# Other buffers, another order of loads and an earlier start for the gate sums of a hybrid decoder layer

## The chip, the cores and the metric

The kernel runs on one core of a Trainium2 chip. The core has a matrix engine (TensorE, "PE" in the profile, with its weight loads as "PEld"), three engines for elementwise work (VectorE "DVE", ScalarE "ACT", GpSimd "POOL") and SyncE ("SP"), which here issues nearly all transfers between the device memory (HBM) and the on-chip memory (SBUF). Each engine works through its own instructions in order; semaphores order them between engines. The metric is the device time of one execution in microseconds (us): lower is better. Times given as "median" are over several executions; the profile shows one execution.

## The reference, cut to what matters

One layer over 512 tokens of width 2048, with a conditioning vector `c`:

```
mod = silu(c) @ w_ada + b_ada              # (1, 3*2048)
shift, scale, gate = split(mod, 3)
h = rms_norm(x, norm_g) * (1 + scale) + shift
u_a, v_a, g_a, q_b, k_b, v_b, g_b, f_b = split(h @ w_in)
y_a = chunked_spatial_gating(gelu(u_a), gelu(v_a), ln_v, w_s, b_s) * silu(g_a)    # branch A
y_b = forgetting_attention(q_b, k_b, v_b, f_b, b_f) * silu(g_b)                    # branch B
y = concat(y_a, y_b) @ w_out
x = x + gate * y
return rms_norm(x, final_g)
```

The change concerns the vector `gate`: 2048 sums over 2048 products of `silu(c)` with the last third of `w_ada` (16 MB of weights). It is not needed before the output projection, near the end.

## The kernel before

**Matrix products.** Everything is float32. A product is made of three passes: each factor is split into a high part (ScalarE rounds, line 131) and a low part (VectorE, or GpSimd in the first stage, subtracts, line 132), and TensorE adds hi x hi, lo x hi and hi x lo. `w_tile` (line 119) makes one weight tile: a buffer of tag `raw` (four buffers of 128 partitions x 4 KB), its load on SP's queue, and the two halves in tags `whi` and `wlo` (two buffers each). `newest_w[0]` (lines 101, 125) always holds the newest such load.

**Stages, in order of time.** (1) shift and scale, `h`, and the first projections beside them, up to about 188 us. (2) `va_products` (line 740): the values of branch A, 16 weight tiles, to about 283 us. (3) the group "ga" (four tiles) and `v_group(0)` (eight half-size tiles), with the spatial mixing of branch A between them. (4) groups of q, k, gate and values of branch B, four tiles each, with the attention of four heads at a time laid between them. (5) the output projection `unit(0)`, `unit(1)`: seven products of half matrices each, in place of eight, which needs sums and differences of quarters of `w_out`. These are made beforehand on GpSimd from loads and written to a scratch tensor `tsum` in HBM: `sum_step(0, k)` for unit 0 (buffers `vs`, `pth`, `ptl`) and `sum_part(1, k, p)` for unit 1 (buffers `wsp`).

**What is laid between.** After each weight tile of stages 2 to 5 the loop calls `tick()` (line 135), which takes one entry of `slots` (attention and mixing steps) and one entry of `fillers`. A tick is thus the time of one weight tile on TensorE and of what is laid in it. Fillers are `spatial_weights`, then eight `sum_step(0, k)` with an empty entry behind each (17 entries: 16 ticks of stage 2 and the first of "ga"). In stage 4 come the gate sums: 32 calls of `gate_step(g, i)` (line 596; `g` one of four column blocks, `i` one of eight pairs of row blocks), with `gate_sum(g)` (line 660) some steps after the last of its block; then the 16 `sum_part` calls.

**The gate steps.** `gate_step` takes a buffer of tag `raw`, loads 512 KB of `w_ada` on SP, and on GpSimd does for each of two row blocks a product with `silu(c)` (line 605, or 603 for the first) and an addition to `gate` (line 606). `gate_sum` adds the 128 partitions with a matrix of ones on TensorE and adds the bias, from a tile `bg` of tag `raw`.

**Order.** The Tile framework orders the instructions of each engine when the program is built: by priority (the order of the program, which `high_priority` shifts ahead; `w_tile` does), by the readiness that a model of time gives, and by free buffers. A tile of a tag waits for one of the tag's buffers to come free. `tc.issue_after(ins)` puts what is traced in it behind `ins` in the queue of that engine. Nothing in the queue of SP overtakes anything: a transfer that waits for a buffer holds up all behind it.

**The buffers `wsp`.** Two of 4 KB per partition. First they hold the split spatial weights (`wsp[0]` for the mixing of heads 0 to 3, `wsp[1]` for 4 to 7, line 777), later the tiles of `sum_part`, and in `unit(1)` two result tiles.

Of the kernel before, what the change touches and what calls it, by code (L numbers as in the profile page):

```python
# [8 lines left out]
F32 = mybir.dt.float32  # L9
# [6 lines left out]
P = 128  # L16
# [11 lines left out]
def trunk_kernel(  # L28
# [17 lines left out]
    nc = tc.nc  # L46

    ada_r = w_ada[0].rearrange("(kb p) (s n) -> p kb s n", p=P, s=3)
# [5 lines left out]
    wp = ctx.enter_context(tc.tile_pool(name="wp", bufs=2))  # L54
# [4 lines left out]
    def bank(tag, name):  # L59
        if tag == "x":  # L60
            tag = "bbbc"[turn[0] % 4]
            turn[0] += 1
        return ps.tile([P, 512], F32, tag=tag, name=name, bufs={"mm": 4, "b": 3, "c": 1}[tag])
# [37 lines left out]
    newest_w = [None]  # L101
# [12 lines left out]
    fillers = []  # L114
# [102 lines left out]
    gate = gp_.tile([P, 4, 512], F32, name="gate")  # L217
# [141 lines left out]
    for q, (k0, nk) in enumerate(CH):  # L359
# [10 lines left out]
        for si, sid in enumerate(order):  # L370
# [9 lines left out]
            for kk in range(k0, k0 + nk, st_k):  # L380
                for gi, (segs, bl) in enumerate(grp):
                    hi, lo = w_tile(
                        segs, kk, st_k, name=f"st{q}_{sid}_{gi}_{kk}", pri=0,
# [29 lines left out]
    pb = ctx.enter_context(tc.tile_pool(name="pb", bufs=1))  # L413
# [15 lines left out]
    wsp = [pb.tile([P, 4, 2, P], F32R, name=f"wsp{i}", tag="wsp", bufs=2) for i in range(2)]  # L429
# [163 lines left out]
        split(fsplit[:, 0, :], fsplit[:, 1, :], f3)  # L593


    def gate_step(g, i):
        ga = wp.tile([P, 2, 512], F32, tag="raw", name=f"gate{g}_{i}", bufs=4)
        nc.sync.dma_start(ga, ada_r[:, 2 * i : 2 * i + 2, 2, g * 512 : (g + 1) * 512])
        for j in range(2):
            kk = 2 * i + j  # L600
            a = gate[:, g, :]
            if kk == 0:
                nc.gpsimd.tensor_scalar(a, ga[:, j], sc[:, 0:1], None, ALU.mult)
            else:
                nc.gpsimd.tensor_scalar(ga[:, j], ga[:, j], sc[:, kk : kk + 1], None, ALU.mult)  # L605
                nc.gpsimd.tensor_tensor(a, a, ga[:, j], ALU.add)  # L606
# [8 lines left out]
    def sum_step(u, k):  # L615

        js = slice((k % 2) * 512, (k % 2) * 512 + 512)
        w = wout_r[:, :, u * 1024 : (u + 1) * 1024].rearrange("p k (s n) -> p k s n", s=2)
        if k % 2:
            a = [pb.tile([P, 2, 512], F32, tag=t, name=f"ts{t}{u}_{k}") for t in ("pth", "ptl")]  # L620
        else:
            o = pb.tile([P, 4, 512], F32, tag="vs", name=f"ts{u}_{k}")
            a = [o[:, 0:2, :], o[:, 2:4, :]]
        nc.sync.dma_start(a[0], w[:, 8 + k])
        nc.sync.dma_start(a[1], w[:, k])
        b11, b12, b21, b22 = (a[z // 2][:, z % 2, :] for z in range(4))
        for z, (dst, l, r) in enumerate((
            (b11, b12, b11), (b12, b12, b22), (b22, b22, b11), (b21, b21, b22),
        )):
            nc.gpsimd.tensor_tensor(dst, l, r, ALU.subtract)  # L630
        if k % 2:
            nc.sync.dma_start(tsum[u][k // 2][:, 0:2, js], a[0])
            nc.sync.dma_start(tsum[u][k // 2][:, 2:4, js], a[1])
        else:
            nc.sync.dma_start(tsum[u][k // 2][:, :, js], o)
# [24 lines left out]
    def gate_sum(g):  # L660
        gsl = slice(2 * D + g * 512, 2 * D + (g + 1) * 512)
        bg = wp.tile([P, 512], F32, name=f"bg{g}", tag="raw", bufs=4)
        nc.sync.dma_start(bg, b_ada[:, gsl].broadcast_to([P, 512]))
        gp = bank("x", f"gp{g}")
        nc.tensor.matmul(gp, ones, gate[:, g, :], start=True, stop=True)
        nc.vector.tensor_tensor(gate[:, g, :], gp, bg, ALU.add)
# [73 lines left out]
    def va_products():  # L740
        va.extend([[pb.tile([P, 512], F32, tag="qstk", bufs=8, name=f"va{t}_{g}") for g in range(2)] for t in range(NT)])
        vst = [pb.tile([P, 2, 6], F32, name=f"vst{t}") for t in range(NT)]
        for g in range(2):
            banks = [bank("x" if g else "mm", f"va{g}_{t}") for t in range(NT)]
            for k in range(0, KB, 2):
                hi, lo = w_tile([(V0 + g * 512, 512)], k, 2, name=f"va{g}_{k}")
                mm_toks(banks, 512, hi, lo, hh, hl, [k, k + 1], 0, KB - 1)
                tick()
            for t in range(NT):
                nc.scalar.activation(va[t][g], banks[t], AF.Gelu)  # L750
                nc.vector.bn_stats(vst[t][:, g, :], va[t][g])
        for t in range(NT):
            mv = pb.tile([P, 2], F32, name=f"mv{t}")
            nc.vector.bn_aggr(mv, vst[t].rearrange("p a b -> p (a b)"))
            rs_ = pb.tile([P, 1], F32, name=f"rsv{t}")
            rsqrt_of(rs_, mv[:, 1:2], 1.0)
            mvs.append(mv)
            rvs.append(rs_)
# [37 lines left out]

    fillers.append(spatial_weights)
    for k in range(8):
        fillers.extend([lambda k=k: sum_step(0, k), lambda: None])
    va_products()  # L800
    slots.extend([
        [c_(norm_half, 0)],
# [9 lines left out]
    gates = []  # L812
    for g in range(4):
        for i in range(8):
            gates.append(lambda g=g, i=i: gate_step(g, i))
            if g and i == 2:
                gates.append(lambda g=g: gate_sum(g - 1))
    gates.extend([lambda: None] * 2 + [lambda: gate_sum(3)])
    parts = [lambda k=k, p=p: sum_part(1, k, p) for k in range(8) for p in range(2)]
    n = 0  # L820
# [330 lines left out]
```

## Time and profile before

| | |
|---|---|
| time, median of 3 executions | 909.44 us (907.97 to 909.47) |
| the profiled execution: time | 907.83 us |
| the profiled execution: span, first to last instruction | 906.1 us |
| granted TensorE clock, mean | 0.986 of full speed |
| matmul instructions | 4408 |
| HBM read and written | 166.90 MB and 20.97 MB |

The profile page gives each engine's busy time, the span in 40 slices with the busy tenths of each, and groups of instructions by line. Beside the page, views of the trace answer narrower questions: stretches (busy time of every engine from A to B us), waits (which engine stood still, at which line, and what released it), the timeline (instructions one by one, with idle time before them and its releaser in brackets), and groups by line in a stretch. In "x<-y" x is written and y read. A matmul is drawn with a modelled end, longer than the distance to the next start, so starts tell more than ends do. The mean over the span hides the stages: each has its own bound.

The DMA slices and what the sums move:

```profile
DMA  9999997338996164544554546676676236577575
gate<-in_w_ada_dram SPq DMA_DIRECT2D x32, 512.0 KB
```

A slice is 22.65 us: the DMA engines are full in the first six, to about 136 us, dense again from the tenth to the thirteenth (stage 2 and what follows, 204 to 294 us), and at four to six tenths in most of stage 4.

### The profile page before, as it was taken

Reading aid. Unit: us, or ns where it says so; the run is one execution under the profiler, and the core shown is the slowest. Engines: PE = TensorE matmul, PEld = TensorE weight load, DVE = VectorE, ACT = ScalarE, POOL = GpSimd, SP = SyncE. Lnnn points to the kernel's source line nnn. Section 1 sums busy time; section 2 is a strip of 40 time slices with the busy share of each in tenths; the row PEclk is TensorE's granted clock in tenths of the full one; section 3 lists DMA queues with packets and bytes.
Section 4 is the critical chain, followed back from the end, with each engine's and each line's share of the span. In section 5 each row is a group of like instructions: output and inputs, shape, how many; then the busy total and the mean of one; then the engine's idle time right before and its main releaser. Section 6 shows DMA issues by size and latency. Waiting matters only on the chain.

```text
span 906.1 us, 12687 instructions
## 1 busy us (share of the span) xinstructions
PE 880.7 (97%) x4408; PEld 745.3 (82%) x4408; DVE 593.8 (66%) x982; ACT 445.5 (49%) x775; POOL 436.9 (48%) x338
## 2 busy tenths in 40 slices
PE   6999999999999999999999999999999999999995
PEld 4888888887888997778789888998897888888884
DVE  4758888473436866454686563447764679996687
ACT  5554332452213324455666554557465657655454
POOL 2365655425576359889998879444651000000001
PEclk7899999999999999999999999999999999999998
DMA  9999997338996164544554546676676236577575
GB/s 340 323 340 357 354 328 222 110 113 292 311 323 201 38 182 125 163 153 136 167 160 141 177 129 186 198 232 191 203 240 203 74 113 213 185 252 245 178 235 205
DMA packets 139712, 188.91 MB, mean 208 GB/s; under 512 B 9968, under 2 KB 103360, under 8 KB 139136
## 3 DMA queue, kind: packets, MB, share of 16 engines
q1 hardware_dynamic: 139216, 187.53, 65.0%
q8 instruction: 35, 0.57, 0.3%
q10 hardware_dynamic: 432, 0.57, 0.2%
q14 instruction: 29, 0.24, 0.1%
HBM read 166.90 MB, written 20.97 MB: 207 GB/s over the span
## 4 chain that ended last, share of the span: by engine, by line
PE 85%; DMA 5%; DVE 4%; issue 2%; ACT 2%; POOL 1%; SPq 0%; POOLq 0%; ACTq 0%; DVEq 0%
PE s L147 6%; PE s L149 6%; PE s L148 6%; PE vb L156 3%; PE vb L157 3%; PE vb L158 3%; PE va L158 3%; PE va L157 3%; PE va L156 3%; PE gb L149 3%; PE gb L148 3%; PE gb L147 3%; PE q L149 3%; PE q L148 3%; PE k L149 3%; PE q L147 3%
## 5 line engine op out<-in xcount | busy, mean ns | idle before, releaser
L605 POOL TENSOR_SCALAR gate<-gate,sc 128x512 f32<-128x512 f32 x60 | 106.4, 1784 | 23.9 <-DMA gate<-in_w_ada_dram 14.9
L132 POOL TENSOR_TENSOR wlo_st<-raw_st,whi_st 128x1024 fp32r<-128x1024 f32 (+3 forms) x36 | 68.4, 1904 | 54.2 <-ACT whi_st L131 48.0
L606 POOL TENSOR_TENSOR gate<-gate,gate 128x512 f32<-128x512 f32 x60 | 92.9, 1550 | 1.8
L147 PE MATMUL s<-hh,whi_st 128*128 128x512 f32 x224 | 88.0, 396 | 1.4 <-ACT hh L269 1.4
L148 PE MATMUL s<-hl,whi_st 128*128 128x512 f32 x224 | 87.8, 392 | 0.0
L651 POOL TENSOR_TENSOR ts<-ts 128x256 f32<-128x256 f32 x64 | 55.1, 866 | 60.4 <-DMA ts<-in_w_out_dram 57.6
L66 ACT ACTIVATE whi_p<-p 128x1024 fp32r<-128x1024 f32 x52 | 55.1, 1060 | 54.8 <-PE woZ L935 20.1
L246 DVE SCALAR_TENSOR_TENSOR acc<-ada,sc,acc 128x512 f32<-128x512 f32 x98 | 73.9, 754 | 4.9 <-DMA ada<-in_w_ada_dram 2.1
L67 DVE TENSOR_TENSOR wlo_p<-p,whi_p 128x1024 fp32r<-128x1024 f32 x52 | 63.4, 1220 | 20.2 <-ACT whi_p L66 20.1
L149 PE MATMUL s<-hh,wlo_st 128*128 128x512 f32 x224 | 76.0, 393 | 0.0
L157 PE MATMUL vb<-whi_vb,hl 128*128 128x256 f32 (+1 forms) x256 | 72.2, 285 | 0.0
L156 PE MATMUL vb<-whi_vb,hh 128*128 128x256 f32 (+1 forms) x256 | 72.0, 285 | 0.0
L158 PE MATMUL vb<-wlo_vb,hh 128*128 128x256 f32 (+1 forms) x256 | 71.3, 288 | 0.0
L978 POOL TENSOR_TENSOR sfin<-sfin,nhalf 128x1 f32<-128x1 f32 x2 | 1.5, 751 | 137.5 <-DVE sfin L1070 137.5
L131 ACT ACTIVATE whi_st<-raw_st 128x1024 fp32r<-128x1024 f32 (+3 forms) x36 | 31.2, 870 | 65.2 <-PE s L148 39.7
L147 PE MATMUL q<-hh,whi_q 128*128 128x512 f32 x128 | 50.6, 395 | 1.2 <-ACT whi_q L131 1.2
L147 PEld LDWEIGHTS s<-hh,whi_st 128*128 128x128 f32 x224 | 42.6, 191 | 10.1 <-ACT hh L269 1.5
L147 PE MATMUL k<-hh,whi_k 128*128 128x512 f32 x128 | 50.2, 392 | 0.7 <-ACT whi_k L131 0.7
L147 PE MATMUL gb<-hh,whi_gb 128*128 128x512 f32 x128 | 50.3, 393 | 0.5 <-ACT whi_gb L131 0.5
L156 PE MATMUL va<-whi_va,hh 128*128 128x512 f32 x128 | 50.3, 393 | 0.0
L148 PE MATMUL gb<-hl,whi_gb 128*128 128x512 f32 x128 | 50.2, 392 | 0.0
L148 PE MATMUL q<-hl,whi_q 128*128 128x512 f32 x128 | 50.2, 392 | 0.0
(308 smaller groups left out, 2523.4 us busy)
## 6 DMA issues: line engine op xcount, KB each, us to landing
ada<-in_w_ada_dram SPq DMA_DIRECT2D x128, 256.0 KB
gate<-in_w_ada_dram SPq DMA_DIRECT2D x32, 512.0 KB
p<-ts SPq DMA_DIRECT2D x32, 512.0 KB
p<-in_w_out_dram SPq DMA_DIRECT2D x24, 512.0 KB
raw_va<-in_w_in_dram SPq DMA_DIRECT2D x16, 512.0 KB
raw_q<-in_w_in_dram SPq DMA_DIRECT2D x16, 512.0 KB
raw_k<-in_w_in_dram SPq DMA_DIRECT2D x16, 512.0 KB
raw_gb<-in_w_in_dram SPq DMA_DIRECT2D x16, 512.0 KB
```

The source lines that it names most:

```text
L66: a = nc.scalar.activation(hi, src, AF.Copy)
L67: return a, (eng or nc.vector).tensor_tensor(lo, src, hi.bitcast(F32), ALU.subtract)
L132: (loeng or nc.vector).tensor_tensor(lo, raw, hi.bitcast(F32), ALU.subtract)
L147: nc.tensor.matmul(pt, hi[:, j, cs], hh[k], start=(k == first), stop=False)
L148: nc.tensor.matmul(pt, hi[:, j, cs], hl[k], start=False, stop=False)
L149: nc.tensor.matmul(pt, lo[:, j, cs], hh[k], start=False, stop=(k == last))
L156: nc.tensor.matmul(o, ah[k][:, tsl], hi[:, j, :], start=(k == first), stop=False)
L157: nc.tensor.matmul(o, al[k][:, tsl], hi[:, j, :], start=False, stop=False)
L158: nc.tensor.matmul(o, ah[k][:, tsl], lo[:, j, :], start=False, stop=(k == last))
L246: nc.vector.scalar_tensor_tensor(sb if kk == KB - 1 else a, ga[:, j], col, a, ALU.mult, ALU.add)
L605: nc.gpsimd.tensor_scalar(ga[:, j], ga[:, j], sc[:, kk : kk + 1], None, ALU.mult)
L606: nc.gpsimd.tensor_tensor(a, a, ga[:, j], ALU.add)
```

## The change

`gate_step` takes its tile from the two `wsp` buffers in place of the four `raw` ones, unless it is called as early; and its load, early or not, is put behind the newest weight load of that moment in SP's queue. The first four steps (`g` 0, `i` 0 to 3) are called early: they take the empty entries behind every second `sum_step(0, k)`, in the values of branch A, and stay in `raw`. The list of gate work in stage 4 then has 28 steps; every fourth entry is a `gate_sum` or empty. It has 40 entries, two more than before, so the `sum_part` calls come two ticks later.

```diff
--- before.py
+++ after.py
@@ -593,9 +593,13 @@
         split(fsplit[:, 0, :], fsplit[:, 1, :], f3)
 
 
-    def gate_step(g, i):
-        ga = wp.tile([P, 2, 512], F32, tag="raw", name=f"gate{g}_{i}", bufs=4)
-        nc.sync.dma_start(ga, ada_r[:, 2 * i : 2 * i + 2, 2, g * 512 : (g + 1) * 512])
+    def gate_step(g, i, early=False):
+        if early:
+            ga = wp.tile([P, 2, 512], F32, tag="raw", name=f"gate{g}_{i}", bufs=4)
+        else:
+            ga = pb.tile([P, 2, 512], F32, tag="wsp", name=f"gate{g}_{i}", bufs=2)
+        with tc.issue_after(newest_w[0].ins):
+            nc.sync.dma_start(ga, ada_r[:, 2 * i : 2 * i + 2, 2, g * 512 : (g + 1) * 512])
         for j in range(2):
             kk = 2 * i + j
             a = gate[:, g, :]
@@ -796,7 +800,8 @@
 
     fillers.append(spatial_weights)
     for k in range(8):
-        fillers.extend([lambda k=k: sum_step(0, k), lambda: None])
+        fillers.append(lambda k=k: sum_step(0, k))
+        fillers.append((lambda k=k: gate_step(0, k // 2, True)) if k % 2 else (lambda: None))
     va_products()
     slots.extend([
         [c_(norm_half, 0)],
@@ -812,9 +817,10 @@
     gates = []
     for g in range(4):
         for i in range(8):
-            gates.append(lambda g=g, i=i: gate_step(g, i))
-            if g and i == 2:
-                gates.append(lambda g=g: gate_sum(g - 1))
+            if g or i > 3:
+                gates.append(lambda g=g, i=i: gate_step(g, i))
+                if len(gates) % 4 == 3:
+                    gates.append((lambda g=g: gate_sum(g - 1)) if g and i in (2, 3, 4) else (lambda: None))
     gates.extend([lambda: None] * 2 + [lambda: gate_sum(3)])
     parts = [lambda k=k, p=p: sum_part(1, k, p) for k in range(8) for p in range(2)]
     n = 0
```

## The prediction

> **What bounds the kernel now.** First the page's busy row and its slices.
>
> ```profile
> span 906.1 us, 12687 instructions
> PE 880.7 (97%) x4408; PEld 745.3 (82%) x4408; DVE 593.8 (66%) x982; ACT 445.5 (49%) x775; POOL 436.9 (48%) x338
> PE   6999999999999999999999999999999999999995
> POOL 2365655425576359889998879444651000000001
> ```
>
> TensorE (PE) is the bound: 906.1 - 880.7 = 25.4 us are not drawn busy, most of them at both ends, where this change does nothing. POOL, idle half the time on average, stands at 8 and 9 tenths in one stretch only, from about 340 to 560 us, where the gate sums run. So next the view of stretches: the branch A values with the weight differences (205 to 285), the mixing (284 to 326), and the gate sums in two halves. Columns: length; PE, PEld, DVE, ACT and POOL busy with counts; clock; DMA share and GB/s.
>
> ```profile
> 205.00:285.00 80.00, 80.00 (x353) 65.53 (x352) 31.13 (x39) 21.49 (x25) 49.45 (x34) 1.00 0.89 304
> 284.00:326.00 42.00, 42.00 (x264) 38.17 (x263) 35.92 (x67) 12.78 (x20) 16.06 (x22) 1.00 0.30 76
> 340.00:460.00 120.00, 115.85 (x522) 93.02 (x521) 71.15 (x106) 61.16 (x114) 109.37 (x69) 1.00 0.49 153
> 460.00:580.00 120.00, 120.00 (x663) 104.70 (x662) 68.97 (x125) 66.95 (x134) 96.98 (x67) 1.00 0.52 157
> ```
>
> PE loses 120 - 115.85 = 4.15 us between 340 and 460 and nothing visible in the other stretches; POOL is 91% busy there, and DMA only half. The view of waits, for PE from 320 to 600 and for SP's queue from 320 to 580, names the late ones (total, times, longest):
>
> ```profile
> PE o L541 <- DVE ptl L67: 1.2, 2, 0.9
> PE q L147 <- ACT whi_q L131: 1.2, 1, 1.2
> PE k L147 <- ACT whi_k L131: 0.7, 1, 0.7
> PE gb L147 <- ACT whi_gb L131: 0.5, 1, 0.5
> PE k L149 <- DVE wlo_k L132: 0.3, 1, 0.3
> PE s L486 <- ACT s L492: 0.2, 1, 0.2
> ...
> SPq L125 <- POOL gate L606: 51.3, 18, 8.0
> SPq L598 <- POOL gate L606: 23.4, 7, 8.1
> ```
>
> PE waits for the halves of the weights (L131, L132), and SP waits 51.3 us, in 18 weight loads, for a gate sum on POOL to give back a `raw` buffer. One case on the timelines of SP and of ACT:
>
> ```profile
> 397.45 0.37 SPq L598 DMA_DIRECT2D gate<-in_w_ada_dram  x1
> 397.91 0.42 SPq L125 DMA_DIRECT2D raw_gb<-in_w_in_dram  x1
> ...
> 403.00 1.06 ACT L131 ACTIVATE whi_gb<-raw_gb 128x1024 fp32r<-128x1024 f32 x1 [3.64 <-DMA raw_gb<-in_w_in_dram]
> ```
>
> The last `raw_gb` goes out at 397.91, behind a gate load, and lands for ACT at 403.00, after PE wanted it. Two of four `raw` buffers hold gate tiles, so weights are loaded about one tile ahead, not three.
>
> What a wait costs is more than its drawn gap:
>
> ```profile
> 364.91 0.39 PE L149 MATMUL k<-hh,wlo_k 128*128 128x512 f32 x1
> 366.04 0.50 PE L147 MATMUL k<-hh,whi_k 128*128 128x512 f32 x1 [0.74 <-ACT whi_k L131]
> 366.38 0.40 PE L148 MATMUL k<-hl,whi_k 128*128 128x512 f32 x1
> 366.61 0.39 PE L147 MATMUL k<-hh,whi_k 128*128 128x512 f32 x1
> ```
>
> Undisturbed, the next matmul starts 0.23 us later (366.38 to 366.61). Here it starts 1.13 later, then 0.34 later: 0.90 + 0.11 = 1.01 us lost against 0.74 drawn, 0.27 more. The PE rows above are seven waits with 4.1 us together; with 7 x 0.27 = 1.9 that makes **6.0 us** that late weights, and the DVE and ACT work held up behind them, cost. The bounds of what can be regained are 0 and 6.0, plus about 1.5 for waits too short to be drawn as gaps.
>
> **The change part by part.**
>
> *Gate tiles leave the four `raw` buffers (28 of 32 steps).* No instruction is removed or added. The 28 loads go to `wsp`. Its two buffers hold the spatial weights until the mixing is done, which POOL's wait shows to be at 324.5, and the first gate load of before stands behind that:
>
> ```profile
> 324.50 1.92 POOL L424 MEMSET k<- 128x512 f32 x4 [14.42 <-PE mix L784]
> 325.84 0.37 SPq L598 DMA_DIRECT2D gate<-in_w_ada_dram  x1
> ```
>
> Weights keep all four `raw` buffers but for four `bg` tiles, so L125's 51.3 us behind POOL goes by construction, and weight loads run up to three tiles ahead. What the steps cost on POOL, and when (the last row has minimum, median and maximum, then first and last start):
>
> ```profile
> L605 POOL TENSOR_SCALAR gate<-gate,sc 128x512 f32<-128x512 f32 x60 | 106.4, 1784 | 23.9 <-DMA gate<-in_w_ada_dram 14.9 <-issue 6.1 <-DVE vs L67 2.3
> L606 POOL TENSOR_TENSOR gate<-gate,gate 128x512 f32<-128x512 f32 x60 | 92.9, 1550 | 1.8
> L605 POOL TENSOR_SCALAR gate<-gate,sc x60: 1560/1569/2638, 331.4 to 563.5; 128x512 f32<-128x512 f32 x60
> ```
>
> A step is 2 x (1.784 + 1.550) = 6.67 us. The 32 steps and three gate sums are 35 ticks between 330 and 567 us, 6.8 us a tick: a tick with a step fills POOL to 98%, and a delay stays. After the change three of four ticks carry one: 5.0 us a tick, 74%. So POOL keeps up, and a gate load should seldom find both `wsp` buffers taken. I take five sixths of the 6.0 us as regained, -5.0; one sixth stays because waits such as that of scores on exp (L486, 0.2) and some lateness in DVE's order are not the loads' doing. Bounds: 0 to -7.5.
>
> *Loads behind weight loads.* Each gate load now stands behind the newest weight load on SP, so the order at 397.45 (gate, then weight) turns round. Behind a waiting gate load stand the next weight load, the q and k rows from `fsplit` and the eight `lt` copies. With three weight tiles loaded ahead, a gate load may wait some 5 us before PE feels it. Valued at nothing; without that cover it is the first rival.
>
> *Four steps into the branch A values (early, still in `raw`).* They add to 205 to 300 us: POOL 4 x 6.67 minus one L606 = 25.1 us at most, and 4 x 0.5 MB of DMA. POOL has 80 - 49.45 = 30.55 us free up to 285, and 42 - 16.06 = 25.9 in the next stretch. For the DMA, 304 GB/s is in use; the best stretch of the trace shows what is to be had:
>
> ```profile
> 60.00:80.00 20.00, 20.00 (x94) 16.66 (x93) 14.48 (x23) 9.96 (x14) 11.02 (x6) 1.00 1.09 355
> ...
> 272.80 1.06 ACT L131 ACTIVATE whi_va<-raw_va 128x1024 fp32r<-128x1024 f32 x1 [4.38 <-PE va L157]
> ...
> 261.41 1.07 SPq L125 DMA_DIRECT2D raw_va<-in_w_in_dram  x1
> ...
> SPq L635 <- POOL ts L630: 20.0, 4, 6.4
> ```
>
> 80 us x 51 GB/s = 4.1 MB are free against 2.1 MB added. The weight that goes out at 261.41 is first read at 272.80, 11.4 us later, and ACT waits for PE there and not for the load: PE sets the pace. The two halves take 1.06 + 1.56 us of a tick of 4.38 + 1.06 = 5.44, so 2.8 us more are spare. One `raw` buffer less makes the lead one tick shorter, 6.0 us, and a load of 0.5 MB at 304 GB/s takes 1.7 alone. SP stands up to 6.4 us at a store of the differences until POOL is done, with weight loads behind it; a step of 6.67 in front would about double that, still inside 6.0 + 2.8. Cost taken: 0. Bounds: 0 to +12 (the second rival); not below 0, as PE loses nothing there now.
>
> Here a rule of the Trainium skill speaks against moving POOL work. Two rows first: the split of a weight on DVE in the branch A stretch, and late in the kernel, where POOL rests.
>
> ```profile
> L132 DVE TENSOR_TENSOR wlo_va<-raw_va,whi_va 128x1024 fp32r<-128x1024 f32 x13 | 20.3, 1564 | 39.6 <-ACT whi_va L131 35.4 <-DMA raw_va<-in_w_in_dram 4.1
> L132 DVE TENSOR_TENSOR wlo_gb<-raw_gb,whi_gb 128x1024 fp32r<-128x1024 f32 x5 | 6.1, 1218 | 2.7 <-PE o L541 2.3 <-ACT whi_gb L131 0.4
> ```
>
> POOL's company makes the mean split 1.564 - 1.218 = 0.35 us longer. (The Trainium skill, "SBUF — State Buffer", section "SBUF: two separate sides", says that a VectorE operation with two SBUF inputs and a GpSimd operation exclude each other for a whole instruction. The trace agrees in kind; by that rule a split can be held for a whole POOL instruction, and the third rival gives its time.) By the rows a split must be 2.8 us late before PE feels it, and none is near.
>
> *Two more ticks.* The list of gate work is 40 entries long, not 38, so the 16 `sum_part` steps start and end two ticks later; the last store falls due three ticks ahead of the end of the projections. They share `wsp` with the gate tiles, but POOL does both in order. 0. Each gate sum comes three ticks or more after its last step: 0.
>
> **Sum**: -5.0 + 0 + 0 + 0. The profiled execution took 907.83 (its span and 1.73 around it) and would take 902.8. It is 1.6 under the median of the runs, 909.44; the forecast for the median is 909.44 - 5.0 = **904.4**.
>
> **The rivals.**
>
> *The wait moves to the gate loads.* Two buffers, POOL at 74% or more with DVE's company, and SP in order: a gate load that waits holds up weights and `lt`. For it: L598 waits 23.4 us in 7 already. Against it: three weight tiles in hand. If such waits keep their share, 23.4 / 74.7 = 31% of 6.0, and double, 3.8 us stay: gain 2.2, **907.2**. A variant has the `lt` copies as the next late thing:
>
> ```profile
> 420.97 6.31 SPq L509 DMA_DIRECT2D q<-lt  x8
> PE t L526 <- DMA q<-lt: 2.3, 2, 2.1
> ```
>
> Eight copies hold SP for 6.31 us, and PE has waited for them twice, later on. If they take back all that is regained ahead of 427 (1.7 drawn, 2.8 with what hides), and the wait for `whi_q` behind them (1.2 drawn, 1.5) stays, the gain is 1.7: **907.7**.
>
> *POOL's order in the branch A stretch (slower).* The differences are a loop of load, POOL, store. If the four steps do not fall into its idle time but in its loop, its end slips by up to 25 us, and ahead of what POOL owes the mixing:
>
> ```profile
> 277.71 1.29 POOL L630 TENSOR_TENSOR tsptl<-tsptl 128x512 f32<-128x512 f32 x1
> 282.87 1.08 POOL L91 TENSOR_TENSOR rsv<-rsv,nhalf 128x1 f32<-128x1 f32 x2 [3.87 <-DVE rsv L90]
> ...
> 293.96 0.69 DVE L67 TENSOR_TENSOR vl<-va,vh 128x512 fp32r<-128x512 f32 x1
> 294.73 0.22 PE L784 MATMUL mix<-wsp,vl 128*128 128x128 f32 x1
> ```
>
> The last difference ends at 279.0, and the first power for the norm runs at 282.87: 3.9 us of cover. The last `vl` (294.65) is done 0.08 us before PE takes it, so beyond 3.9 us PE stands still for each us of slip, unless its order was made otherwise. The kernel turns slower from a slip of 3.9 + 5.0 = 8.9 us; half of the 25, 12, gives +8 - 5 = +3: **912.4**. Against it: DMA waits leave 30 us of POOL free.
>
> *DVE held in the branch A stretch.* If POOL's instructions (up to 2.6 us) hold a split twice in a row, 5.2 - 2.8 = 2.4 us is lost at each; at two of four steps +4.8: 909.2, no difference.
>
> **How the numbers follow.** A difference under 0.2%, 1.8 us, can't be told from none. Chances: forecast 0.55 (902 to 907); the moved wait 0.17 (0.10 of it faster, 0.07 the same); its `lt` variant 0.10 (same); DVE held 0.03 (same); POOL's order 0.15 (slower). So faster 0.65, same 0.20, slower 0.15. For 8 in 10 the range goes from 901.5 (all 7.5 regained, 0.4 below) to 911.0, which leaves out the upper half of the slower case and more.
>
> **What would show it.** Right: no weight load (L125) waits for POOL's gate; PE loses under 1 us drawn from 340 to 460; POOL is busy about 90 of these 120 us instead of 109; gate work shows from about 215 us, with POOL busy near 70 of 205 to 285, and PE full there and at the mixing. Wrong: SP's waits at L598 over 50 us with weight loads late behind them; PE waits at L526 for `lt`, or at L783 and L784 for `vl`; `whi_va` waiting for its load.

## The result and the profile after

| | before | after |
|---|---|---|
| median of 14 executions each, side by side | 907.19 us | 913.86 us |
| lowest and highest | 902.33 and 914.97 | 911.39 and 922.58 |
| the profiled execution: time | 907.83 us | 913.93 us |
| the profiled execution: span | 906.1 us | 912.2 us |

The changed kernel is slower: 1.0085 times the time before, interval [1.0062, 1.0109] (worked out from the single executions; the quotient of the two medians is 1.0074). The forecast was 904.4 us, the range 901.5 to 911.0; it started from 909.44 us, the median of three executions of the kernel before, for which 14 give 907.19. Both profiled executions lie close to their medians, so the 6.1 us between their spans can be followed. (The profiled executions of three of the experiments, e3, e6 and e11, ran their first 34 us at half clock and are some 8 us longer for that alone; stages are therefore compared behind 190 us, and whole kernels by all their executions.)

The page of the changed kernel, with the rows that answer to those of before:

```profile
span 912.2 us, 12659 instructions
PE 882.8 (97%) x4408; PEld 749.0 (82%) x4408; DVE 594.7 (65%) x982; ACT 446.6 (49%) x775; POOL 432.0 (47%) x338
PE   6999999999998999999999999999997999999995
POOL 1355655428788548787887855144652000000001
PEclk7899999999999999999999999999998999999998
```

TensorE is still the bound, and it now has two thinner slices: the 13th (274 to 296 us) and the 31st (684 to 707 us); in the 31st the clock row is down too. Line numbers are four higher after the change (the gate loads L602, the gate additions L610, the differences L634, the mixing L787). The view of waits, for PE from 180 to 770 us, where the columns are total, times and longest:

```profile
PE t L526 <- DMA q<-lt: 5.3, 1, 5.3
PE ga L149 <- DVE wlo_ga L132: 2.5, 1, 2.5
PE mix L787 <- ACT vh L66: 1.7, 1, 1.7
PE k L147 <- ACT whi_k L131: 0.8, 1, 0.8
```

Of the seven waits of before between 320 and 600 us, four of them for halves of weights, one short wait is left (0.8 us). New are 4.2 us at the mixing; and the wait for the `lt` copies of the last four heads is 5.3 us long instead of 2.1 (`lt` holds what normalizes the softmax of four heads; eight small transfers copy its rows into the tiles of q). To see what each costs in all, the starts of TensorE's first products of a group are compared, as they stand on its timeline (a start of before, a start of after, the stage between two starts):

| stage, from and to the first product of | before, us | after, us | difference |
|---|---|---|---|
| begin to "ga" (branch A values are in it) | 283.71 | 283.40 | -0.3 |
| "ga" to the first `vb` (the mixing) | 25.58 | 32.47 | **+6.9** |
| first `vb` to the first `q` | 27.72 | 27.73 | 0 |
| first `q` to the last `gb` (the gate sums) | 351.32 | 345.32 | **-6.0** |
| last `gb` to the output projection (the last heads) | 55.82 | 61.32 | **+5.5** |
| output projection to the end | 161.96 | 161.97 | 0 |

So what was forecast came, one us more than forecast: -6.0. Two stages that were valued at nothing took 12.4 back. The 0.3 us of the first row arose ahead of the change: from the first product of `va` to that of "ga" both kernels take 89.78 us (193.93 to 283.71 and 193.62 to 283.40).

**The mixing.** POOL's timeline in the branch A stretch, first of before: start, duration, then the instruction, and in brackets the idle time ahead of it and its releaser.

```profile
229.31 1.30 POOL L630 TENSOR_TENSOR ts<-ts 128x512 f32<-128x512 f32 x1 [7.45 <-DMA ts<-in_w_out_dram]
231.16 4.41 POOL L630 TENSOR_TENSOR ts<-ts 128x512 f32<-128x512 f32 x3 [0.55 <-DMA ts<-in_w_out_dram]
...
240.50 1.30 POOL L630 TENSOR_TENSOR tsptl<-tsptl 128x512 f32<-128x512 f32 x1
246.66 1.29 POOL L630 TENSOR_TENSOR ts<-ts 128x512 f32<-128x512 f32 x1 [4.87 <-DMA ts<-in_w_out_dram]
```

And of after:

```profile
234.47 1.30 POOL L634 TENSOR_TENSOR ts<-ts 128x512 f32<-128x512 f32 x1
235.74 2.27 POOL L610 TENSOR_TENSOR gate<-gate,gate 128x512 f32<-128x512 f32 x1
...
251.84 2.37 POOL L634 TENSOR_TENSOR tspth<-tspth 128x512 f32<-128x512 f32 x1 [5.33 <-DMA tspth<-in_w_out_dram]
254.89 3.12 POOL L609 TENSOR_SCALAR gate<-gate,sc 128x512 f32<-128x512 f32 x2 [0.69 <-DMA gate<-in_w_ada_dram]
257.96 1.68 POOL L634 TENSOR_TENSOR ts<-ts 128x512 f32<-128x512 f32 x1
...
288.51 1.28 POOL L634 TENSOR_TENSOR tsptl<-tsptl,tspth 128x512 f32<-128x512 f32 x1
289.75 1.19 POOL L91 TENSOR_TENSOR rsv<-rsv,nhalf 128x1 f32<-128x1 f32 x2
290.81 1.27 POOL L634 TENSOR_TENSOR tsptl<-tsptl 128x512 f32<-128x512 f32 x1
```

A round of the differences (two `sum_step` calls: loads, POOL, stores, then the next loads into the buffers that came free) took 246.66 - 229.31 = 17.4 us, with 0.55 + 4.87 = 5.4 us in which POOL waited for loads. With one gate step in it, a round takes 257.96 - 234.47 = 23.5 us, and POOL still waits 5.33 + 0.69 = 6.0 us. In this round the step did not fill the wait; it was added to the round (6.67 us long by the prediction's rows, 6.1 more measured), and the wait moved along behind it. Over the whole loop, from the first difference to the end of the last, part of the wait was filled: POOL's waits fall from 21.0 to 12.6 us, but with 24.1 us of gate work in it the loop takes 81.9 us instead of 70.8. The last difference ends at 292.1 instead of 279.0, 13.1 us late, and the first powers for the norm (L91, reciprocal square roots) at 289.75 instead of 282.87, 6.9 us late. What hangs on them, on the timelines of DVE and then of PE, after:

```profile
283.60 0.21 DVE L758 BATCH_NORM_AGGREGATE mv<-vst 128x2 f32<-128x12 f32 x1
290.36 2.00 DVE L769 TENSOR_SCALAR va<-va,mv,rsv 128x512 f32<-128x512 f32 x2 [6.55 <-POOL rsv L91]
...
293.26 1.21 DVE L132 TENSOR_TENSOR wlo_ga<-raw_ga,whi_ga 128x1024 fp32r<-128x1024 f32 x1
```

```profile
291.62 0.39 PE L787 MATMUL mix<-wsp,vh 128*128 128x256 f32 x1 [1.71 <-ACT vh L66]
294.52 0.79 PE L149 MATMUL ga<-hh,wlo_ga 128*128 128x512 f32 x1 [2.51 <-DVE wlo_ga L132]
295.11 0.63 PE L147 MATMUL ga<-hh,whi_ga 128*128 128x512 f32 x1
295.54 0.63 PE L148 MATMUL ga<-hl,whi_ga 128*128 128x512 f32 x1
```

DVE stood 6.55 us for the power, and the split of a weight of "ga" stands behind that norm work in DVE's order; so PE waits not only for the values to be mixed but also for the low half of a weight. The last two rows show a second price: products start 0.43 us apart (295.11 to 295.54) instead of 0.23, because the granted clock is 0.50 from 292.36 to 299.19. In all 4.2 us drawn became 6.9.

**The last heads.** SP's timeline of before, then of after:

```profile
688.86 0.52 SPq L656 DMA_DIRECT2D ts<-ts  x1
689.44 1.72 SPq L125 DMA_DIRECT2D raw_gb<-in_w_in_dram  x2
691.26 6.06 SPq L509 DMA_DIRECT2D q<-lt  x8
```

```profile
693.62 0.52 SPq L660 DMA_DIRECT2D ts<-ts  x1
694.23 0.57 SPq L125 DMA_DIRECT2D raw_gb<-in_w_in_dram  x1
696.88 0.52 SPq L660 DMA_DIRECT2D ts<-ts  x1
697.45 5.31 SPq L509 DMA_DIRECT2D q<-lt  x8
```

The first `lt` copy goes out 2.9 us behind the last `gb` group's first product before (691.26 - 688.33), and 8.5 us behind it after (697.45 - 688.92). A store of a difference of `w_out`, which waits for POOL until 696.88, stands in front of it. The wait of PE for `lt` grows from 2.1 to 5.3 us, and the clock is at half from 698.55 to 705.38, 4.9 us of it behind the wait.

### The profile page after: what moved, and what is told of

Same layout as the page of the kernel before. It is cut to its first block, busy times and chain, and to the rows that moved or that the text cites. A ratio compares the mean times of both kernels' runs of the same rounds, so it can differ in the third digit from the quotient of the medians.

```text
span 912.2 us, 12659 instructions
## 1 busy us (share of the span) xinstructions
PE 882.8 (97%) x4408; PEld 749.0 (82%) x4408; DVE 594.7 (65%) x982; ACT 446.6 (49%) x775; POOL 432.0 (47%) x338
## 4 chain that ended last, share of the span: by engine, by line
PE 72%; DMA 11%; POOL 7%; DVE 5%; issue 3%; ACT 1%; SPq 1%; POOLq 0%; ACTq 0%; DVEq 0%
DMA ts<-in_w_out_dram 6%; PE s L147 6%; PE s L149 6%; PE s L148 6%; DMA ts<-ts 4%; POOL ts L655 4%; PE gb L149 3%; PE gb L147 3%; PE gb L148 3%; PE q L149 2%; PE q L147 2%; PE q L148 2%; PE k L149 2%; PE k L147 2%; PE k L148 2%
## 5 line engine op out<-in xcount | busy, mean ns | idle before, releaser
L609 POOL TENSOR_SCALAR gate<-gate,sc 128x512 f32<-128x512 f32 x60 | 102.6, 1721 | 44.5 <-DMA gate<-in_w_ada_dram 39.6
L610 POOL TENSOR_TENSOR gate<-gate,gate 128x512 f32<-128x512 f32 x60 | 94.0, 1566 | 2.2
L149 PE MATMUL gb<-hh,wlo_gb 128*128 128x512 f32 x128 | 50.9, 399 | 0.0
```

The lines of the kernel that those rows point to most:

```text
L149: nc.tensor.matmul(pt, lo[:, j, cs], hh[k], start=False, stop=(k == last))
```

## The experiments

Ratios are to the kernel before beside them on the same chip, with 95% intervals; they are worked out from the single executions, not from the two medians given with them. Edits are shown against the changed kernel. The stage times are those of the table above: mixing (25.58 before, 32.47 after), gate sums (351.32, 345.32), last heads (55.82, 61.32).

**e1: the change without the early steps**, all 32 steps in `wsp` behind weight loads, the list of 38 entries as before.

```diff
-        fillers.append((lambda k=k: gate_step(0, k // 2, True)) if k % 2 else (lambda: None))
+        fillers.append(lambda: None)
...
-            if g or i > 3:
-                gates.append(lambda g=g, i=i: gate_step(g, i))
-                if len(gates) % 4 == 3:
-                    gates.append((lambda g=g: gate_sum(g - 1)) if g and i in (2, 3, 4) else (lambda: None))
+            gates.append(lambda g=g, i=i: gate_step(g, i))
+            if g and i == 2:
+                gates.append(lambda g=g: gate_sum(g - 1))
```

> All 32 gate steps stay behind the branch A values, in the two buffers of the weight differences, with the list of 38 entries as before; no step is early. Theory (POOL's order and the late copies): both stalls of the changed kernel go, the gate stage keeps its gain. TensorE starts the values of branch B at 309 us as before (not 316), gains 4 to 6 us between there and 660 us, and waits for the lt copies of the last four heads about as long as before (2 us): about 6 us under the kernel before, ratio 0.993. Rival (the two buffers are the trouble: SP stands at gate loads): the gate stage loses its gain as well, since POOL now has a step on every tick; ratio 1.000 or above.

900.4 against 908.5 us: 0.9933 [0.9893, 0.9974]. Stages 25.57, 345.31, 53.48. The first line is all that is left of PE's waits from 180 to 770 us; the second is SP's, from 320 to 580:

```profile
PE k L149 <- DVE wlo_k L132: 0.8, 2, 0.6
```

```profile
SPq L602 <- POOL gate L610: 79.9, 23, 8.5
```

The whole gain of the gate stage comes without the early steps, and the loss at the mixing goes with them. SP stands 79.9 us at gate loads that wait for POOL, more than the 74.7 at both kinds of load before, and all that is late for PE are two low halves of weights, 0.8 us in all: what stands behind a waiting gate load was needed later still. The first rival (the wait moves to the gate loads) needed just these waits to cost PE, and they cost it hardly anything.

**e3: the changed kernel with a list of 38 entries**, two empty ones taken out, so that the last differences come as early as before.

```diff
+    for z in (7, 3):
+        gates.pop(z)
```

> The changed kernel with two empty entries taken out of the list of gate work, so that the sums for unit 1 start two ticks sooner, as before. Theory (the lt copies of the last four heads stand on SP behind loads and stores of those sums): the wait at 695 us falls from 5.3 us to about 2, the slow matmuls behind it go, the stall at the mixing stays: about 5 us under the changed kernel, ratio to before 1.002. Rival (the copies are late because the gate tiles and the sums now share two buffers): the wait stays at 5 us, ratio 1.008.

912.2 against 908.5 us: 1.001 [0.9967, 1.0054]. Stages 32.60, 347.14, 53.48. PE's waits for `lt` are gone, those at the mixing are the same:

```profile
PE ga L149 <- DVE wlo_ga L132: 2.5, 1, 2.5
PE mix L787 <- ACT vh L66: 1.4, 1, 1.4
```

The first `lt` copy goes out at 698.67, 0.3 us ahead of the last `gb` group's first product (698.94), and no longer 8.5 us behind it. The last heads take 53.48 us, 7.8 less than after the change, for two entries that did nothing. Part of it goes back in the gate stage (+1.8).

**e4: the changed kernel with every gate tile in the four `raw` buffers.**

```diff
-    def gate_step(g, i, early=False):
+    def gate_step(g, i, early=True):
```

> The changed kernel with all 32 gate tiles back in the raw buffers; the early steps, the list of 40 entries and the order behind the weight loads stay. Theory (the gain of the gate stage comes from the buffers alone): TensorE loses again 4 us or more, drawn, in the gate stage; both stalls stay; ratio to before 1.012 to 1.015. Rival (the gain comes from the four steps fewer and the free fourth ticks): the gate stage keeps its gain, ratio 1.008.

913.53 against 908.5 us: 1.0053 [1.001, 1.0096]. Stages 33.4, 346.7, 59.2. From 320 to 580 us SP waits as follows:

```profile
SPq L602 <- POOL gate L610: 63.2, 13, 7.2
SPq L125 <- POOL gate L610: 48.5, 13, 6.8
```

An expectation missed: weight loads wait for the gate sums as long as before (48.5 against 51.3 us), yet 4.6 of the 6.0 us are regained. What is left in this kernel, beside the order, which regains nothing alone (e6), is the thinner work, 28 steps in 37 entries instead of 32 in 35, with no wait of a weight load over 6.8 us instead of 8.0. So other buffers are one remedy of the late weights, not the only one. That the thinner work is the other is argued, not shown: no run has it alone.

**e5: three early steps**, the fourth moved to the head of the list in stage 4.

```diff
-        fillers.append((lambda k=k: gate_step(0, k // 2, True)) if k % 2 else (lambda: None))
+        fillers.append((lambda k=k: gate_step(0, k // 2, True)) if k in (1, 3, 5) else (lambda: None))
...
+    gates.pop(3)
+    gates.insert(0, lambda: gate_step(0, 3))
```

> The changed kernel with three early steps in place of four; the fourth, which ran on POOL from 274 to 281 us ahead of the last difference, is the first of the list behind and takes the place of an empty entry, so that the list keeps its 40 entries. Theory (POOL's order): the last difference ends some 6 us sooner, the powers for the norm run at about 284 us and not 290, and the stall at the mixing, 6.9 us by the starts of the next group, falls under 2; the wait for the lt copies stays at 5; ratio to before 1.001 to 1.003. Rival (any POOL work or DMA added there slows the loop of differences, whatever its place): at least half of the stall stays, ratio 1.005 or above.

913.73 against 908.5 us: 1.0055 [1.0014, 1.0095]. Stages 32.88, 345.5, 58.77. The theory that the fourth step, the one just in front of the last round of differences, makes the stall fell. POOL's timeline:

```profile
280.62 4.03 POOL L634 TENSOR_TENSOR ts<-ts 128x512 f32<-128x512 f32 x3 [9.52 <-DMA ts<-in_w_out_dram]
...
288.35 1.19 POOL L91 TENSOR_TENSOR rsv<-rsv,nhalf 128x1 f32<-128x1 f32 x2
```

Where the fourth step was, POOL now waits 9.52 us for the loads of the last round, and begins it at 280.62 where the changed kernel had 281.87; counted from the first product of "ga" (281.61 and 283.40) that is 0.5 us later. The loop takes 83.4 us with only 15.4 us of gate work in it: the three rounds before have already made it late.

**e6: the order alone**, gate loads behind weight loads, tiles in `raw`, no early step, 38 entries.

```diff
-    def gate_step(g, i, early=False):
+    def gate_step(g, i, early=True):
...
-        fillers.append((lambda k=k: gate_step(0, k // 2, True)) if k % 2 else (lambda: None))
+        fillers.append(lambda: None)
...
+            gates.append(lambda g=g, i=i: gate_step(g, i))
+            if g and i == 2:
+                gates.append(lambda g=g: gate_sum(g - 1))
```

> The kernel before with one edit: each gate load is put behind the newest weight load on SP. All gate tiles stay in the raw buffers, no step is early, the list is the old one of 38 entries. The run with all tiles in raw kept 4.6 of the 6.0 us that the gate stage gained, so the buffers alone are not the cause. Theory now (the order on SP makes most of the gain): the stage from the first q group to the last gate group takes 4 us or more less than before (351.3 us), ratio 0.995 or below. Rival (it was the four steps fewer and the free ticks): the stage takes as long as before within 1.5 us, ratio 1.000.

907.0 against 907.33 us: 0.9988 [0.9942, 1.0033], no difference. Stages 25.57, 353.37, 55.06: the theory fell, by itself the order regains nothing of the gate stage.

**e7: the buffers alone**, `wsp` without the order, no early step, 38 entries.

```diff
-        with tc.issue_after(newest_w[0].ins):
+        with ExitStack() as es:
...
-        fillers.append((lambda k=k: gate_step(0, k // 2, True)) if k % 2 else (lambda: None))
+        fillers.append(lambda: None)
...
+            gates.append(lambda g=g, i=i: gate_step(g, i))
+            if g and i == 2:
+                gates.append(lambda g=g: gate_sum(g - 1))
```

> The kernel before with the other edit: all 32 gate tiles in the two buffers of the weight differences, but no order behind the weight loads; no early step, the old list. Theory (order): the gate loads again stand ahead of weight loads, but a weight has three tiles of lead, so half of the gain or more is still there: 345 to 348 us for the stage. Rival (buffers are all of it): the full gain, 345.5 us or less. If both edits do the same thing, each alone gives nearly all of it, and together no more than 6.0.

901.81 against 907.33 us: 0.9928 [0.989, 0.9966]. Stages 25.57, 346.91, 54.88. The buffers regain 4.4 of the 6.0 us; the order adds 1.6 where the buffers are there (345.31 in e1), and nothing without them. The 1.6 are read from one profile each; the ratios of the whole kernels (0.9928 here, 0.9933 in e1) do not tell the two apart.

**e8: the loads of the early steps without their arithmetic on POOL**; ScalarE reads each tile instead.

```diff
+            if early:
+                if kk == 0:
+                    nc.gpsimd.memset(a, 0.0)
+                nc.scalar.activation(b1[0:1, 0:1], ga[0:1, j, 0:1], AF.Copy)
-            if kk == 0:
+            elif kk == 0:
```

> The changed kernel with the arithmetic of the four early steps on POOL left out (gate block 0 lacks its first eight products); their loads, buffers and places stay, and ScalarE reads one element of each. Theory (POOL's time in the loop of differences): the last difference ends within 3 us of the kernel before (279 us), and from the first tile of the ga group to the first of the values of branch B TensorE takes 26 us as before and not 32.5. Rival (the loads on SP and in the DMA queue slow the loop): at least 29 us.

One time, 911.7 us. Stages 25.57, 345.64, 59.25, but "ga" begins 5.4 us later than before (289.07): PE waits once in the values of branch A.

```profile
PE va L156 <- ACT whi_va L131: 3.8, 1, 3.8
```

It is inconclusive for TensorE, since the reading made a stall of its own: ScalarE stood 12.33 us, until 280.45, at a gate tile that had not landed, with the split of the late weight behind it in its order, and the clock was at half from 282.04 to 285.45. The mixing shows no stall, as all of TensorE is late with the differences. On POOL, the loads without the arithmetic do lengthen the loop: the last difference ends at 284.63, which is 91.0 us behind the first product of `va` (193.62) where it was 85.1 before, 5.9 us late and not within 3 as expected. How much of that the reading on ScalarE added is not known.

**e9: the arithmetic of the early steps without their loads**; POOL reads a tile that is there.

```diff
-        with tc.issue_after(newest_w[0].ins):
-            nc.sync.dma_start(ga, ada_r[:, 2 * i : 2 * i + 2, 2, g * 512 : (g + 1) * 512])
+        if not early:
+            with tc.issue_after(newest_w[0].ins):
+                nc.sync.dma_start(ga, ada_r[:, 2 * i : 2 * i + 2, 2, g * 512 : (g + 1) * 512])
...
+            src = hh[0].bitcast(F32) if early else ga[:, j]
-                nc.gpsimd.tensor_scalar(a, ga[:, j], sc[:, 0:1], None, ALU.mult)
+                nc.gpsimd.tensor_scalar(a, src, sc[:, 0:1], None, ALU.mult)
...
```

> The changed kernel with the loads of the four early steps left out; POOL does the same operations on a tile that is there already (gate block 0 gets another tile in place of its first eight row blocks). Theory (POOL's time): the loop of differences still slips by 6 us a round, last difference at 288 us or later, 31 to 33 us from ga to the values of branch B. Rival (the loads): 26 to 28 us. If the two together make the stall (each step waits in POOL's order for its own load, with the differences behind it), both runs come out under 29.

One time, 905.48 us. Stages 25.57, 345.66, 60.69. On POOL's timeline the last difference ends at 282.8, 3.8 us later than before, and the powers come at their old time; but this execution came to branch A 1.3 us sooner:

```profile
279.17 3.64 POOL L636 TENSOR_TENSOR ts<-ts 128x512 f32<-128x512 f32 x2
282.77 1.19 POOL L91 TENSOR_TENSOR rsv<-rsv,nhalf 128x1 f32<-128x1 f32 x2
```

Counted from the first product of `va` (192.61 here, 193.93 before, 193.62 after), the last difference ends 90.2 us later, where before had 85.1 and the changed kernel 98.5. So with the four steps' arithmetic on POOL, but no loads, the slip is 5.1 us instead of 13.4, the powers are 1.2 us late, and TensorE loses nothing at the mixing. A part of it was easier than in the changed kernel: the first step began at 201 us, ahead of the first difference, where with a load it had to wait until 206.00. The theory (288 us or later) fell; what was expected of the two together, both runs under 29 us at the mixing, came (25.57 in both, for e8 with its own stall ahead of it). Neither the arithmetic alone (5.1) nor the loads alone (5.9, with e8's reservation) slip as far as both together (13.4). Whether the loads alone would cost TensorE anything is left open by e8.

**e10: three early steps, and the norm powers ahead of the last differences** in POOL's order; the list has 38 entries.

```diff
...
-                nc.gpsimd.tensor_tensor(dst, l, r, ALU.subtract)
+                with ExitStack() as es:
+                    if k > 5:
+                        es.enter_context(tc.issue_after(powers[-1].ins))
+                    nc.gpsimd.tensor_tensor(dst, l, r, ALU.subtract)
...
-            rsqrt_of(rs_, mv[:, 1:2], 1.0)
+            powers.append(rsqrt_of(rs_, mv[:, 1:2], 1.0))
...
+        if k == 6:
+            fillers.extend([lambda: None] * 3)
...
+    for z in (15, 7, 3):
+        gates.pop(z)
+    gates.insert(0, lambda: gate_step(0, 3))
```

> The changed kernel with POOL's order mended: the last two sum steps of unit 0 come behind the powers for the norm on POOL, three early steps stay and the fourth goes behind; the list has 38 entries. Theory (the mixing waits because the powers stand on POOL behind the late differences, and the lt copies because the list is two ticks longer): 26 us from ga to the values of branch B as before, no wait for lt over 1 us, the gate stage keeps its 6 us: ratio to before 0.992 to 0.994. Rival (the loads of the early steps also make weights of the ga group late): 28 us or more from ga to the values of branch B, ratio 0.996 or above.

905.84 against 906.84 us: 0.9983 [0.9948, 1.0018], no difference. Stages 30.03, 349.28, 53.48. POOL's timeline, then PE's waits:

```profile
281.97 1.09 POOL L91 TENSOR_TENSOR rsv<-rsv,nhalf 128x1 f32<-128x1 f32 x2 [10.95 <-DVE rsv L90]
```

```profile
PE mix L792 <- DVE vl L67: 2.5, 1, 2.5
PE k L150 <- DVE wlo_k L133: 1.7, 2, 1.2
PE k L148 <- ACT whi_k L132: 1.1, 1, 1.1
```

The powers are on time (281.97), and the wait for them is gone. But the expected 26 us and 0.992 to 0.994 did not come. Of the 6.9 us at the mixing 4.5 stay, now as a wait for `vl`: the two norm operations on DVE ahead of it (L773, from 291.63) took 6.43 us where the same two took 1.47 before (from 292.53), and POOL worked on four differences between 291.57 and 297.78. PE's wait is 2.5 us, and 3.41 us at half clock follow from 300.35. The gate stage keeps only 2.0 of its gain: two waits of 1.1 and 1.2 us for halves of a `k` weight, near 370 us, and 3.41 us at half clock from 372.03. So the place of the powers explains a part; the differences, moved behind them, now ran beside DVE's norm work, which took 5.0 us longer; and no way was found in which the early steps paid.

**e11: e1 once more**, beside e10.

> The kernel without early steps once more, beside the one above on the same chip: ratio 0.993 again. If the early steps are worth anything once their two stalls are gone, the kernel above is faster than this one by 0.2% or more; if not, the two agree within 0.2%.

899.07 against 906.84 us: 0.9917 [0.9889, 0.9945]. Stages 25.57, 345.22, 54.1. This version, the change without its early steps, beats both kernels.

## Why the prediction was wrong

*Gate tiles leave the raw buffers: right, a little small.* -5.0 was taken as five sixths of the 6.0 us that late weights cost; 6.0 came back, so the sixth held back for other causes was not needed. The sum of 6.0 for the drawn waits, with 0.27 us added to each, comes out to the tenth, and that is partly luck: one wait of 0.8 us is still there, so some of what came back must be waits too short to be drawn, for which the bounds had 1.5. The cause that was given, buffers, is right (e7, 4.4) but not alone (e4, 4.6 with none of it).

*Loads behind weight loads: valued at nothing, right in the kernel as a whole.* e6 shows no difference for the order alone; beside the buffers it brings 1.6 us.

*Four steps into the branch A values: this step failed.* "Cost taken: 0. Bounds: 0 to +12" ; it cost 6.9. The working counted POOL's 30.55 free us against 25.1 us of work. It did not ask what that free time was: POOL waiting for loads inside a loop. A step that brings a load of its own and has a fixed place in POOL's order lengthened a round from 17.4 to 23.5 us, and the loop from 70.8 to 81.9. The third part of the working, DMA and weights, held: the values of branch A take 89.78 us in both kernels, and PE waits for no `va` weight, so the rival "DVE held" cost nothing there either (in e10, at the mixing, DVE's norm work took 5.0 us longer beside POOL's differences). Its sum was not sound, though: a stand of SP of 6.4 us, doubled, is 13 us and not inside 6.0 + 2.8. It was not needed, as SP stood at most 4.5 us at a store of the differences between 205 and 293 us (L636). The rival "POOL's order in the branch A stretch" had the mechanism, the 3.9 us of cover and nearly the slip (12 taken, 13.1 measured) and was given 0.15. Its statement that PE loses every us beyond the cover is not what was seen: that gives 13.1 - 3.9 = 9.2, and 6.9 came. The powers were 6.9 us late, not 13.1, as POOL's order put them ahead of the last difference; and about 2 of the 6.9 are half clock, which no part of the sum contained: ten products from 294.52 to 298.53 us take 4.0 us instead of 9 x 0.23 = 2.1.

*Two more ticks, taken as 0: this step failed too.* It cost 5.5. It followed POOL's order and the due time of the last store, and not SP's queue, where the last stores stand in front of eight `lt` copies. The variant with `lt` as the next late thing was among the rivals, but was placed at the first heads (421 us); the row that was quoted for it, 2.1 us of waiting, belongs to the last four heads. e3 isolates it: two entries fewer, and the wait is gone. In the seven profiles with lists of 38 entries (before among them) the last heads take 53.5 to 55.8 us, in the five with 40 entries 58.8 to 61.3.

*The signs.* No weight load waits for POOL's gate in stage 4 any more, and PE is nearly full there, but POOL is busier than the 90 us forecast. The stretches 205 to 285, 284 to 326, 340 to 460 and 460 to 580 us, after:

```profile
205.00:285.00 80.00, 80.00 (x353) 65.55 (x352) 31.10 (x35) 21.70 (x25) 66.18 (x43) 1.00 0.87 295
284.00:326.00 42.00, 37.78 (x210) 32.91 (x209) 32.07 (x57) 11.26 (x18) 22.42 (x26) 0.92 0.40 120
340.00:460.00 120.00, 119.10 (x560) 98.55 (x559) 75.09 (x114) 66.00 (x125) 99.36 (x65) 1.00 0.49 155
460.00:580.00 120.00, 120.00 (x662) 104.60 (x661) 66.70 (x124) 66.27 (x134) 77.75 (x53) 1.00 0.42 133
```

PE goes from 115.85 to 119.10 of 120. POOL's two halves together fall from 206.4 to 177.1 us, 29 less, about the four steps that were taken out (26.7); only the share of the first half is higher than three steps in four ticks would make it. POOL at 66.18 in the first stretch was forecast near 70, and PE full there: right. PE at 37.78 of 42 in the second is the sign of the rival, and the wait at L526 that of the `lt` variant.

*The sum.* -0.3 + 6.9 - 6.0 + 5.5 = +6.1 in the profiled executions; +6.7 between the medians. Not settled: how the slip of the differences divides between the loads of the early steps and their arithmetic, since e8 had a stall of its own; and what regains 4.6 us in e4.

## What to carry to other kernels

Before filling the idle time of an engine, ask what it waits for there: idle time inside a loop of load, compute and store is not simply free, and work put into it can lengthen the loop. Here a round went from 17.4 to 23.5 us, and the end of the loop slipped by 13.4 us with four steps and their loads, by 5.1 with their arithmetic alone; only the first cost TensorE time. When a list of work becomes two entries longer, go through every queue that the last entries use, and look for the small transfers that stand behind them. A wait of TensorE of a few us, or two of 1.1 us close together, should be priced with the half clock that can follow it.

## What the hardware showed unexpectedly

The granted clock in three stretches, the first two of the changed kernel (behind the wait for `lt`, and at the mixing), then one of before (behind its wait for `lt`):

```profile
698.55:705.38 6.83, 4.92 (x13) 4.08 (x14) 3.61 (x8) 3.13 (x8) 0.00 (x0) 0.50 0.37 113
292.36:299.19 6.83, 4.67 (x11) 3.70 (x12) 6.83 (x14) 2.21 (x3) 4.05 (x7) 0.50 0.42 129
```

```profile
696.70:704.00 7.30, 7.30 (x34) 6.12 (x35) 4.30 (x11) 4.41 (x10) 0.00 (x0) 1.00 0.49 144
```

After a wait of 5.32 us TensorE runs at half clock until 705.38; after the 2.11 us of before it stays at 1.00. In e4 a wait of 2.58 us, from 695.74 to 698.32, had half clock from 697.78 to 704.61. Each of these three stretches at half clock is 6.83 us long. So the wait of 5.3 us cost some 2.3 more: the four products for `t` took 1.40 instead of 0.83 us, and the eight steps behind them, from 701.66 to 705.18, took 3.52 us where 0.23 each makes 1.84. Other stretches are half as long, 3.41 us: in e5 from 697.17, in e6 from 467.30, in e8 from 282.04, in e10 from 300.35 and 372.03. The Trainium skill, "TensorE: Matmul & The Clock Gate", section "Part 1: The HAM clock gate (the "warmup" mystery)", says that activity in free-running windows of 3413 ns sets the clock, and that it goes to half after at least one idle window. Two such windows are 6.83 us, which agrees. But the 3.41 us ahead of the drop in e4 (694.37 to 697.78) held products for 1.37 us, up to 695.74, so a window that is 60% idle sufficed; here the measurement decides. The waits can be shorter still: in e10 the 3.41 us ahead of 372.03 held one of 1.1 us and all but the end of one of 1.2, with PE drawn busy for 1.44, and in e6 the 3.41 us ahead of 467.30 held none over 1.44 us, with PE drawn busy for 1.63. Between 60 us and the output projection the twelve profiles show thirteen drops to half clock, each behind 3.41 us in which PE was drawn busy for at most 48%. No threshold follows: one such stretch of e1 (886.51 to 889.93), 46% busy, had no drop behind it.
